# A two-layer gated attention trunk: head transposes through the projections' PSUM banks, attention outputs written over the queries, and a last merge ordered by rows

## The chip, the cores and the metric

The kernel runs on one core of one Trainium2 chip. The metric is the device time of one execution in microseconds; the time of the kernel before is 639.28 us, the median of three runs (639.04 to 639.41). One execution was recorded by the hardware profiler; its own time was 638.95 us.

## The reference

Each of two layers normalises 256 rows of 1024 numbers, projects them by `w_in`, and runs three attention branches beside each other: A (8 heads, causal), B (8 heads, each query sees only the 64 keys that an index score picked) and M (4 heads over 256 memory rows). Each branch is gated, lifted to 1024 columns by its own matrix, weighted by a gate of its own and summed; the sum goes through `w_out` and is added to the rows. All arithmetic is in float32. Cut to its core:

```
proj = einsum('bsd,dc->bsc', rmsnorm(x), w_in)
qa, ka, qb, kb, qi, ki = partial_rope(...)             # first 16 of each head's 64 numbers
ya = moba_attention(qa, ka, va) * silu(a_g)            # one block of 256: plain causal attention
yb = dsa_attention(qb, kb, vb, qi, ki, wi) * silu(b_g) # top 64 keys by index score
ym = memory_attention(m_q, km, vm) * silu(m_g)
up = einsum('bsnw,nwd->bsnd', stack([ya, yb, ym]), w_branch)
x  = x + einsum('bsd,de->bse', sum(sigmoid(mix) * up, axis=2), w_out)
```

## The kernel before

Every float32 product is made of three matmuls (`mm3`, L105 to L108): both operands are split into a rounded part and the rest, and high x high, high x low and low x high are summed in PSUM. Weights come in units of 128x1024 numbers (512 KB): a DMA on SyncE's queue into `raw`, ScalarE rounds it into `whi` (L102), VectorE subtracts to get `wlo` (L103), and TensorE uses a unit in 24 matmuls of 512 columns or 48 of 256. TensorE writes into eight PSUM banks in three pools: `pmm` with four (accumulators of projections, and later of the branch matrices), `psa` with two (scores), `pst` with two (transposes).

The order in a layer is: memory keys and values; the index projection (`index_mask`, L394), whose 584 columns for two row tiles take two banks of `pmm` and two of `psa`; the projections M_Q and M_G; memory attention; A_Q, A_K, A_G, attention A with its values; the same for B; then six mixing projections (`mixes`) and six branch products (`merge`); `merged_T`; `w_out`.

For queries and keys a projection is rotated (`rope`: ScalarE copies, VectorE makes three small products, GpSimd adds them at L207 into `qf`), transposed by TensorE into a bank (`heads_T`, L211 to L219, eight transposes in two banks), and split by ScalarE and VectorE into the tile `dst` (L227). The index keys, queries of A and B and keys of A and B go through `heads_T`; in this kernel its banks are from `pst`.

VectorE also carries the index scores, the 16 turns of top-k (MAX8 and MATCH_REPLACE, L441 and L442), the memory scores' row maxima (L369), the splits of transposed probabilities (L385) and the gating of outputs (L390). The framework's scheduler fixes one order of instructions for each engine ahead of the run; an engine waits in that order, and an accumulator's bank is reused only when its readers are done.

`merge` (L539) adds for each of its two weight units both row tiles into two banks, multiplies by the mix on VectorE (L551), and GpSimd adds that to the sum (L553). `merged_T` transposes the sum (L562) and splits it into `mgh` and `mgl` (L564, L565), the left operands of `w_out`.

Of the kernel before, what the change touches and what calls it, by code (L numbers as in the profile page):

```python
# [7 lines left out]
F32 = mybir.dt.float32  # L8
F32R = mybir.dt.float32r
AF = mybir.ActivationFunctionType  # L10
ALU = mybir.AluOpType
PSUM = bass.MemoryType.PSUM

P = 128
D = 1024
S = 256
# [18 lines left out]
def trunk(ctx, tc, x, x_t, mem, mem_t, consts, norm_g, gains, w_grp, w_idx, w_mix, w_kv, w_br, w_o, final_g, out):  # L35
# [1 line left out]

    cp = ctx.enter_context(tc.tile_pool(name="cp", bufs=1))
    wp = ctx.enter_context(tc.tile_pool(name="wp", bufs=4))
    big = ctx.enter_context(tc.tile_pool(name="big", bufs=9))  # L40
    wk = ctx.enter_context(tc.tile_pool(name="wk", bufs=2))
    pmm = ctx.enter_context(tc.tile_pool(name="pmm", bufs=4, space=PSUM))
    psa = ctx.enter_context(tc.tile_pool(name="psa", bufs=2, space=PSUM))
# [2 lines left out]
    def bank(pool, tag):  # L46
        return pool.tile([P, 512], F32, tag=tag, name=tag)
# [4 lines left out]

    gm = cp.tile([P, 2, L, KC], F32, name="gm")
    nc.sync.dma_start(gm, gains)
    memT = cp.tile([P, KC, S], F32, name="memT")
    xr = [cp.tile([P, D], F32, name=f"xr{t}") for t in range(NT)]
    mr = [wk.tile([P, D], F32, tag="h", name="mr", bufs=3) for t in range(NT)]

# [78 lines left out]
    def mem_stats():  # L137
        nc.vector.tensor_copy(rB, rstd_row(mr, rsm))

    def mem_prep(l, mh, ml, ks):  # L140

        for k in ks:
            g = gm[:, 1, l, k:k + 1]
            nc.scalar.activation(mh[:, k, :], memT[:, k, :], AF.Copy, scale=g)
            nc.vector.scalar_tensor_tensor(ml[:, k, :], memT[:, k, :], g, mh[:, k, :].bitcast(F32),
                                           op0=ALU.mult, op1=ALU.subtract)
# [64 lines left out]
    def heads_T(qf, done):  # L211

        for c in range(2):
            pt = bank(pst, "pt")
            for i in range(2):
                for t in range(NT):
                    j = 2 * c + i
                    nc.tensor.transpose(pt[:, i * S + t * P:i * S + (t + 1) * P], qf[t][:, j * P:(j + 1) * P], ident)  # L218
            done(c, pt.rearrange("p (a b) -> p a b", b=S))  # L219
# [99 lines left out]
    def attn_out(p, prs, v, y, s2):  # L319
        pt0 = bank(pst, "pt").rearrange("p (a b) -> p a b", b=S)  # L320
        pt1 = bank(pst, "pt").rearrange("p (a b) -> p a b", b=S)
        for i in range(2):
            for t in range(NT):
                nc.tensor.transpose(pt0[:, i, t * P:(t + 1) * P], prs[t][:, i, 0:P], ident)  # L324
        for i in range(2):
            nc.tensor.transpose(pt1[:, i, 0:P], prs[1][:, i, P:S], ident)
        h0 = wk.tile([P, 2, S], F32R, tag="ph", name="ph")
        l0 = wk.tile([P, 2, S], F32R, tag="pl", name="pl")
        split(h0, l0, pt0)
        b1 = wk.tile([P, 2, 2, P], F32R, tag="pb", name="pb")  # L330
        split(b1[:, :, 0], b1[:, :, 1], pt1[:, :, :P])
        yf = wk.tile([P, S], F32, tag="yf", name="yf")
        for i, pool in enumerate(((psa, "sc"), (pst, "pt"))):

            yp = bank(*pool)
            c = slice((2 * p + i) * P, (2 * p + i + 1) * P)
            nc.tensor.matmul(yp[:, :S], v[:, 0, c], h0[:, i], start=True, stop=False, skip_group_check=True)
            nc.tensor.matmul(yp[:, :S], v[:, 0, c], l0[:, i], start=False, stop=False, skip_group_check=True)
            nc.tensor.matmul(yp[:, P:P + S], v[:, 1, c], b1[:, i].rearrange("p a b -> p (a b)"), start=False, stop=True,
                             skip_group_check=True)  # L340
            r, q = slice(64 * i, 64 * i + 64), slice(64 - 64 * i, 128 - 64 * i)
            nc.scalar.copy(yf[r], yp[q, :S])
            nc.vector.tensor_add(yf[r], yf[r], yp[r, :S])
            nc.vector.tensor_add(yf[r, P:S], yf[r, P:S], yp[r, S:S + P])
        nc.vector.scalar_tensor_tensor(yf, yf, 0.5, s2[:, p * S:(p + 1) * S], op0=ALU.mult, op1=ALU.mult)
        split(y[:, 0, p * S:(p + 1) * S], y[:, 1, p * S:(p + 1) * S], yf)

    def attend(qT, kT, vals, masks, y, s2):
        prs = attn_probs(0, qT, kT, masks)
        v = vals()  # L350
        for p in range(4):
            ahead = attn_probs(p + 1, qT, kT, masks) if p < 3 else None
            attn_out(p, prs, v, y, s2)
            prs = ahead

    def mem_probs(p, qT, kT):
        prs = []
# [118 lines left out]
    mhl = mem_tiles()  # L476
    for l in range(L):
        if l == 0:
            xT = big.tile([P, KC, S], F32, tag="big", name="xT")
            rest = [[], [], [(xr[0], x[0:P, :])], [(xr[1], x[P:S, :])], [(cst, consts), (xT[:, :4], x_t[:, :4])],  # L480
                    [(xT[:, 4:], x_t[:, 4:])], [], []]

            def ahead(u):
                if u < 4:
                    nc.sync.dma_start(memT[:, 2 * u:2 * u + 2, :], mem_t[:, 2 * u:2 * u + 2, :])
                    mem_prep(l, *mhl, range(2 * u, 2 * u + 2))
                for a, b in rest[u]:
                    load_after(a, b)
                if u > 5:
                    for k in range(4 * u - 24, 4 * u - 20):  # L490
                        nc.scalar.activation(xT[:, k, :], xT[:, k, :], AF.Copy, scale=gm[:, 0, 0, k:k + 1])
                if u == 7:
                    normT.extend(normed_first(xT))
# [26 lines left out]
        aq = roped(l, A_Q, hh, hl, queries_T, "aq")  # L520
        ak = roped(l, A_K, hh, hl, keys_T, "ak")
        gate(l, A_G, hh, hl, s2[0])
        yA = two("yA")
        attend(aq, ak, lambda: values(l, A_V, hh, hl, "av"), cmask, yA, s2[0])

        bq = roped(l, B_Q, hh, hl, queries_T, "bq")
        bk = roped(l, B_K, hh, hl, keys_T, "bk")
        gate(l, B_G, hh, hl, s2[1])
        yB = two("yB")
        attend(bq, bk, lambda: values(l, B_V, hh, hl, "bv"), masks, yB, s2[1])  # L530

        def mixes(b, n):

# [5 lines left out]
        def merge(b, n, mx, acc):  # L539

            ups = [bank(pmm, "mm") for _ in range(NT)]
            for u in range(2):
                hi, lo = unit(w_br[l, b, n, :, 2 * u:2 * u + 2, :], 1024)
                for q in range(2):
                    k = 2 * u + q
                    ww = slice(q * 512, (q + 1) * 512)
                    for t in range(NT):
                        yy = slice(k * S + t * P, k * S + (t + 1) * P)
                        mm3(ups[t], ys[n][:, 0, yy], ys[n][:, 1, yy], hi[:, ww], lo[:, ww], k == 0, k == 3)
            for t in range(NT):  # L550
                nc.vector.scalar_tensor_tensor(mx[:, t], mx[:, t], 1.0, ups[t], op0=ALU.add, op1=ALU.mult)  # L551
                if n:
                    nc.gpsimd.tensor_tensor(acc[:, t], acc[:, t], mx[:, t], op=ALU.add)  # L553

        def merged_T(b, acc):

# [10 lines left out]

        mh = big.tile([P, KC, S], F32R, tag="big", name="mgh")
        ml = big.tile([P, KC, S], F32R, tag="big", name="mgl")
        ys = [yA, yM, yB]  # L570

        todo = [(0, 0), (0, 1), (1, 0), (1, 1), (0, 2), (1, 2)]
        mxs = [mixes(*todo[j]) for j in range(3)]
        for j, (b, n) in enumerate(todo):
            if j == 3 and l + 1 < L:
                mhl = mem_tiles()
                mem_prep(l + 1, *mhl, range(KC))
            merge(b, n, mxs[j], mxs[2 * b])
            if j != 2 and len(mxs) < 6:
                mxs.append(mixes(*todo[len(mxs)]))  # L580
            if n == 2:
                merged_T(b, mxs[2 * b])
# [123 lines left out]
```

## Time and profile before

| what | value |
|---|---|
| median of three runs | 639.28 us |
| profiled execution, its own time | 638.95 us |
| its span, first to last instruction | 637.2 us |
| TensorE busy, share of the span | 615.4 us, 97% |
| VectorE busy | 482.0 us, 76% |
| ScalarE busy | 389.5 us, 61% |
| GpSimd busy | 109.8 us, 17% |

The busy time of TensorE counts matmuls, whose ends are modelled; the weight loads run beside them. The granted clock (PEclk) is 1.00 at 2.4 GHz and 0.50 at 1.2 GHz. In rows of the timeline the first number is the start in us from the span's start, the second the duration; what stands in brackets is the idle time just before, and what ended it. A matmul's own duration is longer than the step to the next one, so the pace of matmuls is read from their starts.

### The profile page before, as it was taken

The page shows a single profiled execution, that of the slowest core. Times are in us where ns is not written, and L with a number is a line of the kernel's source. Part 1 is how long each engine was busy: PE and PEld are TensorE (multiplying, and loading weights), DVE is VectorE, ACT ScalarE, POOL GpSimd, SP SyncE. Part 2 cuts the span into 40 slices and gives each one's busy share as a digit, 9 for nine tenths or more (in the row PEclk, how much of TensorE's full clock was granted, in tenths as well). Part 3 has the DMA queues.
Part 4 walks back from the last instruction along what each step waited for, and adds up shares of the span by engine and source line. Part 5 has one row for each costly group of instructions (what it writes and reads, how often), then busy time and mean ns, then how long its engine had stood idle before and what let it go on. Part 6 is the DMA issues. An engine that isn't in the chain of part 4 may idle for free.

```text
span 637.2 us, 10090 instructions
## 1 busy us (share of the span) xinstructions
PE 615.4 (97%) x3518; PEld 537.9 (84%) x3518; DVE 482.0 (76%) x994; ACT 389.5 (61%) x721; POOL 109.8 (17%) x166
## 2 busy tenths in 40 slices
PE   7989999999999999988999999999999999999795
PEld 4989989889988888867889998998898888888684
DVE  5678799987867878965485777998886688877453
ACT  5858656677756867552464666647765577665232
POOL 1303003013110114304010200210321002312222
PEclk9999999999999999998999999999999999999799
DMA  8966554456455455563554855454555464555421
GB/s 301 372 193 229 180 171 148 130 167 193 141 170 164 162 166 167 172 192 95 178 180 126 269 165 169 136 166 156 174 156 165 135 202 159 170 164 173 125 66 67
DMA packets 31587, 108.52 MB, mean 170 GB/s; under 512 B 3632, under 2 KB 3632, under 8 KB 31536
## 3 DMA queue, kind: packets, MB, share of 16 engines
q1 hardware_dynamic: 31248, 107.35, 52.5%
q8 instruction: 28, 0.46, 0.3%
q10 hardware_dynamic: 288, 0.52, 0.2%
q14 instruction: 23, 0.19, 0.1%
HBM read 106.81 MB, written 1.05 MB: 169 GB/s over the span
## 4 chain that ended last, share of the span: by engine, by line
PE 90%; DVE 3%; DMA 2%; issue 1%; POOL 1%; ACT 1%; SPq 0%; POOLq 0%; DVEq 0%; ACTq 0%
PE mm L107 24%; PE mm L106 24%; PE mm L108 24%; PE sc L106 2%; PE sc L108 2%; PE sc L107 2%; PE sc L298 2%; PE pt L218 1%; DVE wlo L103 1%; PE pt L324 1%; PE pt L106 1%; DMA raw<-in_w_kv 1%; PE pt L108 1%; PE pt L107 1%; PE sc L295 1%
## 5 line engine op out<-in xcount | busy, mean ns | idle before, releaser
L103 DVE TENSOR_TENSOR wlo<-raw,whi 128x1024 fp32r<-128x1024 f32 (+2 forms) x201 | 242.0, 1207 | 95.9 <-ACT whi L102 94.2
L102 ACT CAST whi<-raw 128x1024 fp32r<-128x1024 f32 (+2 forms) x201 | 203.8, 1017 | 138.0 <-PE mm L108 67.4
L108 PE MATMUL mm<-whi,hl 128*128 128x512 f32 (+2 forms) x416 | 159.3, 384 | 1.4 <-DVE hl L103 1.4
L106 PE MATMUL mm<-whi,hh 128*128 128x512 f32 (+2 forms) x416 | 159.9, 387 | 0.0
L107 PE MATMUL mm<-wlo,hh 128*128 128x512 f32 (+2 forms) x416 | 159.9, 385 | 0.0
L108 PEld LDWEIGHTS mm<-whi,hl 128*128 128x128 f32 x416 | 78.0, 188 | 16.0 <-DVE hl L103 1.6
L107 PEld LDWEIGHTS mm<-wlo,hh 128*128 128x128 f32 x416 | 78.2, 188 | 13.4
L106 PEld LDWEIGHTS mm<-whi,hh 128*128 128x128 f32 x416 | 77.9, 188 | 13.5
L285 POOL TENSOR_SCALAR pr<-pr,rinv 128x256 f32<-128x256 f32 (+1 forms) x80 | 45.8, 588 | 172.1 <-DVE rinv L283 148.0
L108 PE MATMUL mm<-hh,wlo 128*128 128x256 f32 x256 | 73.0, 286 | 0.3 <-DVE wlo L103 0.3
L107 PE MATMUL mm<-hl,whi 128*128 128x256 f32 x256 | 72.7, 284 | 0.0
L106 PE MATMUL mm<-hh,whi 128*128 128x256 f32 x256 | 72.7, 284 | 0.0
L108 PEld LDWEIGHTS mm<-hh,wlo 128*128 128x128 f32 x256 | 48.9, 191 | 0.5 <-DVE wlo L103 0.5
L106 PEld LDWEIGHTS mm<-hh,whi 128*128 128x128 f32 x256 | 49.0, 191 | 0.1
L107 PEld LDWEIGHTS mm<-hl,whi 128*128 128x128 f32 x256 | 48.9, 191 | 0.1
L207 POOL TENSOR_TENSOR qf<-rt,rt 128x128 f32<-128x128 f32 (+2 forms) x24 | 17.4, 732 | 175.7 <-DVE rt L206 175.7
L280 ACT ACTIVATE pr<-tm,nb 128x128 f32<-128x128 f32 (+1 forms) x80 | 36.7, 460 | 17.0 <-DVE nb L314 13.8
L553 POOL TENSOR_TENSOR mx<-mx 128x512 f32<-128x512 f32 x16 | 28.2, 1778 | 83.5 <-DVE mx L551 83.5
L536 ACT ACTIVATE mx<-mm 128x512 f32<-128x512 f32 x24 | 14.3, 598 | 10.1 <-PE mm L108 9.8
L106 PE MATMUL mm<-mh,whi 128*128 128x256 f32 x64 | 18.1, 284 | 0.0
L107 PE MATMUL mm<-ml,whi 128*128 128x256 f32 x64 | 18.0, 283 | 0.0
L108 PE MATMUL mm<-mh,wlo 128*128 128x256 f32 x64 | 17.9, 284 | 0.0
(257 smaller groups left out, 1130.7 us busy)
## 6 DMA issues: line engine op xcount, KB each, us to landing
raw<-in_w_grp SPq DMA_DIRECT2D x80, 512.0 KB, 4.5
raw<-in_w_mix SPq DMA_DIRECT2D x48, 512.0 KB, 3.9
raw<-in_w_br SPq DMA_DIRECT2D x24, 512.0 KB, 3.8
raw<-in_w_o SPq DMA_DIRECT2D x16, 512.0 KB, 3.6
raw<-in_w_kv SPq DMA_DIRECT2D x15, 512.0 KB, 4.3
raw<-in_w_idx SPq DMA_DIRECT2D x16, 292.0 KB, 3.2
memT<-in_mem_t SPq DMA_DIRECT2D x4, 256.0 KB, 5.7
xr<-in_x SPq DMA_DIRECT2D x2, 512.0 KB, 6.5
```

Of the source, the lines that this page charges most:

```text
L102: nc.scalar.copy(hi, src)
L103: nc.vector.tensor_sub(lo, src, hi.bitcast(F32))
L106: nc.tensor.matmul(o, lh, rh, start=start, stop=False, skip_group_check=True)
L107: nc.tensor.matmul(o, lh, rl, start=False, stop=False, skip_group_check=True)
L108: nc.tensor.matmul(o, ll, rh, start=False, stop=stop, skip_group_check=True)
L207: nc.gpsimd.tensor_tensor(dst[:, :, 0:16], t1[:, :nh], t2[:, :nh], op=ALU.add)
L218: nc.tensor.transpose(pt[:, i * S + t * P:i * S + (t + 1) * P], qf[t][:, j * P:(j + 1) * P], ident)
L280: nc.scalar.activation(pr[:, i, :nk], tm[:, i, :nk], AF.Exp, bias=nb[:, i:i + 1], scale=scale, accum_out=rsum[:, i:i + 1])
L285: nc.gpsimd.tensor_scalar(pr[:, i, :nk], pr[:, i, :nk], rinv[:, i:i + 1], 1.0, op0=ALU.mult, op1=ALU.mult)
L298: nc.tensor.matmul(scs[i][:, 1, :], qT[:, h, P:], k[:, b, :], start=b == 0, stop=b == 1, skip_group_check=True)
L536: lambda t, i, ps: nc.scalar.activation(mx[:, t], ps, AF.Tanh, scale=0.5))
L553: nc.gpsimd.tensor_tensor(acc[:, t], acc[:, t], mx[:, t], op=ALU.add)
```

## The change

Four edits. `heads_T` takes its two banks from `pmm` in place of `pst`. `attend` has no output tile of its own any more: the output y of head pair p is written into slices 2p and 2p+1 of the query tile, and the pool `big` has ten buffers in place of nine. The transposed memory `memT`, loaded once into a buffer of its own, lies in `big`, and is loaded a second time (1 MB) for layer 1 in the middle of layer 0's merges. `merge` takes both weight units first and does all 12 matmuls of row tile 0 before those of row tile 1, and the sum of the last branch is made on VectorE and not on GpSimd.

```diff
-    big = ctx.enter_context(tc.tile_pool(name="big", bufs=9))
+    big = ctx.enter_context(tc.tile_pool(name="big", bufs=10))
...
-    memT = cp.tile([P, KC, S], F32, name="memT")
...
     def heads_T(qf, done):
         for c in range(2):
-            pt = bank(pst, "pt")
+            pt = bank(pmm, "mm")
...
-        split(y[:, 0, p * S:(p + 1) * S], y[:, 1, p * S:(p + 1) * S], yf)
+        split(y(0, p), y(1, p), yf)
...
-    def attend(qT, kT, vals, masks, y, s2):
+    def attend(qT, kT, vals, masks, s2):
+        def y(part, pair):
+            return qT[:, 2 * pair + part, :]
...
-        yA = two("yA")
-        attend(aq, ak, lambda: values(l, A_V, hh, hl, "av"), cmask, yA, s2[0])
+        yA = attend(aq, ak, lambda: values(l, A_V, hh, hl, "av"), cmask, s2[0])
...
             ups = [bank(pmm, "mm") for _ in range(NT)]
-            for u in range(2):
-                hi, lo = unit(w_br[l, b, n, :, 2 * u:2 * u + 2, :], 1024)
-                for q in range(2):
-                    k = 2 * u + q
-                    ww = slice(q * 512, (q + 1) * 512)
-                    for t in range(NT):
-                        yy = slice(k * S + t * P, k * S + (t + 1) * P)
-                        mm3(ups[t], ys[n][:, 0, yy], ys[n][:, 1, yy], hi[:, ww], lo[:, ww], k == 0, k == 3)
+            us = [unit(w_br[l, b, n, :, 2 * u:2 * u + 2, :], 1024) for u in range(2)]
             for t in range(NT):
+                yy = slice(t * P, (t + 1) * P)
+                for k in range(4):
+                    hi, lo = us[k // 2]
+                    ww = slice(k % 2 * 512, (k % 2 + 1) * 512)
+                    mm3(ups[t], ys[n](0, k)[:, yy], ys[n](1, k)[:, yy], hi[:, ww], lo[:, ww], k == 0, k == 3)
                 nc.vector.scalar_tensor_tensor(mx[:, t], mx[:, t], 1.0, ups[t], op0=ALU.add, op1=ALU.mult)
                 if n:
-                    nc.gpsimd.tensor_tensor(acc[:, t], acc[:, t], mx[:, t], op=ALU.add)
+                    (nc.gpsimd, nc.vector)[n - 1].tensor_tensor(acc[:, t], acc[:, t], mx[:, t], op=ALU.add)
...
             if j == 3 and l + 1 < L:
                 mhl = mem_tiles()
-                mem_prep(l + 1, *mhl, range(KC))
+                memT = big.tile([P, KC, S], F32, tag="big", name="memT")
+                load_after(memT, mem_t)
+                mem_prep(l + 1, memT, *mhl, range(KC))
```

The edits move instructions on every engine. Three places on TensorE follow, each before and now (line numbers of the changed file are smaller by one up to `attend`). First, TensorE behind the index projection in layer 0; `qf` is the rotated index query, `hh` and `hl` are the left operands of M_Q. Before:

```order
L106 MATMUL sc<-whi,hh 128x264
L107 MATMUL sc<-wlo,hh 128x264
L108 MATMUL sc<-whi,hl 128x264
L106 MATMUL mm<-hh,whi 128x256
L107 MATMUL mm<-hl,whi 128x256
...
L107 MATMUL mm<-hl,whi 128x256
L218 MATMUL pt<-cst,qf 128x128
L108 MATMUL mm<-hh,wlo 128x256
```

Now:

```order
L105 MATMUL sc<-whi,hh 128x264
L106 MATMUL sc<-wlo,hh 128x264
L107 MATMUL sc<-whi,hl 128x264
L217 MATMUL mm<-cst,qf 128x128 x2
L105 MATMUL mm<-hh,whi 128x256
L106 MATMUL mm<-hl,whi 128x256
```

Before, 29 matmuls of M_Q stand between the index projection's last matmul and the first transpose of `qf`; now two transposes stand directly behind it, and M_Q behind them. In layer 1 the same two transposes stand at the same place.

Second, TensorE ahead of the gate projection A_G in layer 0. `sc_1131` is the memory output of the second head pair, `qf_1166` and `qf_1286` are rotated A queries and A keys, `mm_1583` before is an accumulator of the values, `mm_1415` now is A_G's first accumulator. Before:

```order
L106 MATMUL sc_1131<-ph_1152,vm_110 128x256
L107 MATMUL sc_1131<-pl_1153,vm_110 128x256
L108 MATMUL sc_1131<-ph_1152,vm_110 128x256
L218 MATMUL pt_1268<-cst_83,qf_1166 128x128 x4
L218 MATMUL pt_1277<-cst_83,qf_1166 128x128 x4
L107 MATMUL mm_1583<-wlo_1605,hh_322 128x512
L108 MATMUL mm_1583<-whi_1604,hl_323 128x512
```

Now:

```order
L217 MATMUL mm_1389<-cst_82,qf_1286 128x128 x3
L217 MATMUL mm_1402<-cst_82,qf_1286 128x128 x3
L106 MATMUL sc_1131<-pl_1138,vm_110 128x256
...
L105 MATMUL sc_1131<-ph_1152,vm_110 128x256
L106 MATMUL sc_1131<-pl_1153,vm_110 128x256
L107 MATMUL sc_1131<-ph_1152,vm_110 128x256
L105 MATMUL mm_1415<-hh_322,whi_1418 128x256
L106 MATMUL mm_1415<-hl_323,whi_1418 128x256
```

Before, A_G and the values run among the memory outputs and the transposes; now A_K (48 matmuls of 512 columns) is the last weight work ahead of the memory outputs and both sets of transposes, and A_G's 96 matmuls come in one piece behind all of them. A_G's first accumulator is the bank that held the first half of the A queries' transposes (`mm_1268`, read by VectorE as below).

```order
L444 MAX m8_1358<-work_710 128x8
L102 TENSOR_TENSOR aq_1267<-mm_1268,aq_1267 64x2x256
L102 TENSOR_TENSOR aq_1267<-mm_1277,aq_1267 64x2x256
L445 MATCH_REPLACE work_709<-m8_1337,work_709 128x128
L102 TENSOR_TENSOR ak_1387<-mm_1389,ak_1387 64x2x256
L102 TENSOR_TENSOR ak_1388<-mm_1402,ak_1388 64x2x256
L445 MATCH_REPLACE work_710<-m8_1358,work_710 128x256
L393 SCALAR_TENSOR_TENSOR yf2_1162<-sc_1131,s2_912 128x512
L102 TENSOR_TENSOR aq_1267<-mm_1268,aq_1267 64x2x256
```

These are VectorE's rows now: the second of the two splits that read `mm_1268` stands behind the top-k turns, the key splits and the gating of `sc_1131`, and A_G's first matmul waits for it.

Third, TensorE at the last merge of the first column half in layer 0. Before:

```order
L107 MATMUL mm<-wlo,yB 128x512
L108 MATMUL mm<-whi,yB 128x512 x2
L562 MATMUL mm<-cst,mx 128x128 x8
L106 MATMUL mm<-whi,yB 128x512
L107 MATMUL mm<-wlo,yB 128x512
```

Now (`bq` is the query tile that holds B's output):

```order
L105 MATMUL mm<-whi,bq 128x512
L106 MATMUL mm<-wlo,bq 128x512
L107 MATMUL mm<-whi,bq 128x512
L562 MATMUL mm<-cst,mx 128x128 x4
L105 MATMUL sc<-whi,mgh 128x512
L106 MATMUL sc<-wlo,mgh 128x512
```

Before, eight transposes of the sum follow the branch product at once; now row tile 0's four follow, 12 matmuls of `w_out` stand behind them, and row tile 1's four come after those.

## Rows read from the trace of the kernel before

**Rows 1.** The page: span, TensorE's busy time, the chain by engine.

```profile
span 637.2 us, 10090 instructions
PE 615.4 (97%) x3518; PEld 537.9 (84%) x3518; DVE 482.0 (76%) x994; ACT 389.5 (61%) x721; POOL 109.8 (17%) x166
PE 90%; DVE 3%; DMA 2%; issue 1%; POOL 1%; ACT 1%; SPq 0%; POOLq 0%; DVEq 0%; ACTq 0%
```

**Rows 2.** Timeline of TensorE, layer 0's last merges: start, duration, instruction, idle before.

```profile
281.38 0.39 PE L107 MATMUL mm<-wlo,yB 128*128 128x512 f32 x1
281.61 0.39 PE L108 MATMUL mm<-whi,yB 128*128 128x512 f32 x1
283.98 0.50 PE L106 MATMUL mm<-whi,yB 128*128 128x512 f32 x1 [1.98 <-ACT yB L102]
...
285.01 0.63 PE L108 MATMUL mm<-whi,yB 128*128 128x512 f32 x2
287.60 0.66 PE L562 MATMUL mm<-cst,mx 128*128 128x128 f32 x4 [1.96 <-POOL mx L553]
289.81 1.11 PE L562 MATMUL mm<-cst,mx 128*128 128x128 f32 x4 [1.55 <-POOL mx L553]
```

**Rows 3.** Timeline of TensorE, layer 1's last merges.

```profile
592.95 0.39 PE L108 MATMUL mm<-whi,yB 128*128 128x512 f32 x1
595.19 0.66 PE L562 MATMUL mm<-cst,mx 128*128 128x128 f32 x4 [1.86 <-POOL mx L553]
597.40 1.12 PE L562 MATMUL mm<-cst,mx 128*128 128x128 f32 x4 [1.55 <-POOL mx L553]
```

**Rows 4.** Windows behind those waits: length, busy times, granted clock, DMA share, GB/s.

```profile
290.00:293.00 3.00, 3.00 (x11) 2.53 (x10) 0.69 (x1) 0.60 (x1) 0.00 (x0) 0.56 0.41 152
597.40:603.00 5.60, 5.60 (x15) 4.55 (x16) 0.69 (x1) 0.60 (x1) 0.00 (x0) 0.50 0.23 84
```

**Rows 5.** Timeline of TensorE: first M_Q matmuls in layer 0, then layer 1.

```profile
45.88 0.28 PE L106 MATMUL mm<-hh,whi 128*128 128x256 f32 x1
...
356.75 0.28 PE L106 MATMUL mm<-hh,whi 128*128 128x256 f32 x1
356.87 0.28 PE L107 MATMUL mm<-hl,whi 128*128 128x256 f32 x1
```

**Rows 6.** Timeline of GpSimd: the index queries' rotation, layer 0, then layer 1.

```profile
48.45 1.27 POOL L207 TENSOR_TENSOR qf<-rt,rt 128x80 f32<-128x80 f32 x1 [15.79 <-DVE rt L206]
49.88 1.20 POOL L207 TENSOR_TENSOR qf<-rt,rt 128x48 f32<-128x48 f32 x1 [0.16 <-DVE rt L206]
...
51.67 0.36 POOL L207 TENSOR_TENSOR qf<-rt,rt 128x80 f32<-128x80 f32 x1 [0.21 <-DVE rt L206]
...
358.73 1.59 POOL L207 TENSOR_TENSOR qf<-rt,rt 128x80 f32<-128x80 f32 x2 [33.23 <-DVE rt L206]
```

**Rows 7.** VectorE by line and shape, 88 to 118 us: busy us, mean ns.

```profile
L103 DVE TENSOR_TENSOR wlo<-raw,whi 128x1024 fp32r<-128x1024 f32 x9 | 10.9, 1215 | 0.8 <-ACT whi L102 0.8
L369 DVE CUSTOM_DVE_ANT_0 tm<-sc,rB 128x256 f32<-128x256 f32 x8 | 3.0, 414 | 0.0
L441 DVE MAX8 m<-work 128x8 f32<-128x256 f32 x7 | 2.9, 414 | 0.0
L385 DVE SCALAR_TENSOR_TENSOR pl<-pt,rsm,ph 128x512 fp32r<-128x512 f32 x4 | 2.9, 736 | 0.0
L442 DVE MATCH_REPLACE8 work<-m,work 128x256 f32<-128x256 f32 x7 | 2.9, 408 | 0.0
L441 DVE MAX8 m<-work 128x8 f32<-128x128 f32 x7 | 2.0, 284 | 0.0
L442 DVE MATCH_REPLACE8 work<-m,work 128x128 f32<-128x128 f32 x7 | 1.9, 275 | 0.0
L390 DVE SCALAR_TENSOR_TENSOR yf<-sc,s 128x512 f32<-128x512 f32 x1 | 0.7, 681 | 0.0
```

**Rows 8.** The same 30 us as one window; columns as in rows 4.

```profile
88.00:118.00 30.00, 30.00 (x206) 27.87 (x206) 29.18 (x96) 17.46 (x34) 6.33 (x14) 1.00 0.49 150
```

More of the change, by code (lines that the diff above doesn't have):

```diff
@@ L138, in mem_stats, with mem_prep @@
         nc.vector.tensor_copy(rB, rstd_row(mr, rsm))
-    def mem_prep(l, mh, ml, ks):
+    def mem_prep(l, memT, mh, ml, ks):
         for k in ks:
@@ L354, in attend @@
             prs = ahead
+        return y
     def mem_probs(p, qT, kT):
@@ L485, in ahead @@
                     nc.sync.dma_start(memT[:, 2 * u:2 * u + 2, :], mem_t[:, 2 * u:2 * u + 2, :])
-                    mem_prep(l, *mhl, range(2 * u, 2 * u + 2))
+                    mem_prep(l, memT, *mhl, range(2 * u, 2 * u + 2))
                 for a, b in rest[u]:
@@ L528, in trunk @@
         gate(l, B_G, hh, hl, s2[1])
-        yB = two("yB")
-        attend(bq, bk, lambda: values(l, B_V, hh, hl, "bv"), masks, yB, s2[1])
+        yB = attend(bq, bk, lambda: values(l, B_V, hh, hl, "bv"), masks, s2[1])
         def mixes(b, n):
@@ L569, in trunk @@
         ml = big.tile([P, KC, S], F32R, tag="big", name="mgl")
-        ys = [yA, yM, yB]
+        ys = [yA, lambda part, k: yM[:, part, k * S:(k + 1) * S], yB]
         todo = [(0, 0), (0, 1), (1, 0), (1, 1), (0, 2), (1, 2)]
@@ L576, in trunk @@
                 mhl = mem_tiles()
-                mem_prep(l + 1, *mhl, range(KC))
+                memT = big.tile([P, KC, S], F32, tag="big", name="memT")
+                load_after(memT, mem_t)
+                mem_prep(l + 1, memT, *mhl, range(KC))
             merge(b, n, mxs[j], mxs[2 * b])
```

## The prediction

> **What bounds the kernel now.** I read the page first: TensorE is busy for 615.4 of 637.2 us and the chain that ends last is 90% TensorE [rows 1]. So what counts is whether an edit opens or closes a gap on TensorE; work on the other engines is free while TensorE has matmuls that can run. The idle time is 22 us. The timeline of TensorE puts part of it at the end of each layer. In layer 0 the matmul after the one at 281.61 starts at 283.98, waiting for the last split of yB; with a pace of 0.23 us (281.38 to 281.61) that is 2.14 us lost. Then 285.47 (two matmuls from 285.01) to 287.60 is 2.13 us, and from the end of four transposes (4 x 0.11 us, an estimate from half of a 256-column step) to 289.81 another 1.77, both waiting for GpSimd's sum L553 [rows 2]. Layer 1 has the last two: 2.01 and 1.77 us [rows 3]. Behind these waits the granted clock is 0.56 of full over 3.0 us and 0.50 over 5.6 us, that is 1.2 GHz and not 2.4 GHz for most of the stretch, which costs 3.0 x 0.44 = 1.3 and 5.6 x 0.5 = 2.8 us [rows 4]. Together 7.4 us in layer 0 and 6.6 in layer 1. The other idle time lies in the first 40 us and the last 10, which the change hardly touches.
>
> **The change part by part.** *Last merges and y over the queries: -12 us.* Now B's attention ends before the branch products need it (the outputs need no tile of their own, and VectorE's last split of y comes before the last mixing products), so the wait for yB goes. The sum is made on VectorE, where an instruction over 128x512 takes 0.68 us [rows 7], and under row tile 0's product and sum (1.4 us) lie row tile 1's 12 matmuls, 2.7 us. So both waits for GpSimd go, and the clock drop with them: -14.0 us. What is late next is the split of row tile 0's four transposes: `w_out`'s 12 matmuls stand right behind them, and 0.4 us of transposes and 0.6 us of ScalarE's copy come ahead. I take 1 us per layer, so -12; bounds -14 and -10. Writing y over the queries costs nothing, since a pair's scores are read long before its y comes.
>
> *Index queries through the projections' banks: +8.5 us.* Before, M_Q's first matmul follows the index projection at once, at 45.88 us [rows 5], and 29 of M_Q cover the rotation. Now the first two transposes stand there, and M_Q takes the banks that the index projection leaves. TensorE can't go past a transpose whose `qf` isn't ready, and GpSimd's order there is the old one: its additions end at 48.45 + 1.27 and 49.88 + 1.20 = 51.08 [rows 6]. So TensorE stands from 45.88 to 51.1, 5.2 us, less 0.3 us that it waited there before: 4.9. In layer 1 M_Q starts at 356.75 [rows 5] and the two additions end at 358.73 + 1.59 = 360.32 [rows 6]: 3.6. What covered this, M_Q, now stands behind it. From below: if GpSimd's additions took the 0.36 us that the same shape takes at 51.67 [rows 6], the second, which can't start before 49.88, ends at 50.24, and the stand is 4.4 - 0.3 = 4.1 and some 2.8 us: 6.9 in all. From above 9.
>
> *A's queries and keys through those banks: +16 us.* This is the large term. Before, A_G and the values run among the memory outputs. Now, from the end of A_Q to A_G, TensorE has only A_K (48 matmuls of 0.23 us = 11.0) and 73 short ones (24 memory scores, 24 memory outputs and transposes, nearly all at 0.12 us or under [rows 5]; about 8.4): 19.4 us. A_G's first matmul waits until VectorE has read the bank of A's queries for the second time. VectorE has, from the first memory score to that split: 5 weight splits of 1.215 us (6.1), 8 row maxima of 0.414 (3.3), 8 MAX8 of 0.284 and 8 of 0.414 (5.6), 8 MATCH_REPLACE of 0.275 and 8 of 0.408 (5.5), 4 splits of 0.736 (2.9), 8 of 0.681 (5.4) [rows 7], and 37 small ones of 0.08 to 0.28 us (4.7): 33.5 us. Neighbours overlap: the 26 groups of that answer, of which eight stand in rows 7, sum to 36.0 us where VectorE was busy for 29.18 of 30 us [rows 8], a factor of 0.81. So 27.2 us, and about 1 us until the first score is there (six matmuls and a hand-over, an estimate), against 19.4: TensorE stands 9 us, in pieces, the largest ahead of A_G. In layer 1 the turns of top-k are fewer at that point: 31.9 x 0.81 = 25.8, plus 1, against 57 x 0.23 + 61 x 0.12 = 20.2; 7 us. Together 16. VectorE was 97% busy over the same work before [rows 8] and TensorE still never stood, because it had A_G and the values to run; that cover is what goes. From below: with VectorE quite caught up the last wait stays, as the gating of the second memory output and the split behind it (2 x 0.681 and hand-overs) come after TensorE's last matmul: 1.5 us per layer, 3 in all. From above: without overlap between neighbours the stand is 33.5 + 1 - 19.4 = 15 in layer 0 and 13 in layer 1; I hold 11 each for the practical end, as GpSimd's and ScalarE's hand-overs lie in between. I take 16, by the row nearest to it, the busy share in rows 8.
>
> *B's queries and keys:* the same transposes there wait for `qf` with weight matmuls of the neighbours in between: +1 per layer, 0 to 2.
>
> *The clock:* behind gaps of about 2 us the trace shows 1.3 and 2.8 us lost to 1.2 GHz [rows 4]. There are four new places with a gap of 3 us or more (two behind the index projection, two ahead of A_G): 4 x 1 = 4 us, bounds 0 and 4 x 2.8 = 11. The Trainium skill ("TensorE: Matmul & The Clock Gate", section "What's actually happening") says that the halved clock is the resting state, which activity lifts and idleness brings back; the trace agrees as far as the two places in rows 4 go. By that rule alone each of the four would be sure to pay.
>
> *Memory in common buffers:* eight ScalarE and eight VectorE instructions in layer 0's merges stay, one GpSimd copy and a 1 MB load come in, on SyncE's queue between weight loads. At the 150 GB/s of rows 8 it takes 7 us; the DMA engines are half idle there [rows 8], and ScalarE reaches the eight instructions some five units after the load is issued. I take 0, bounds 0 and 3.
>
> **Sum**, against the profiled execution (span 637.2 [rows 1] plus 1.75 around it, 638.95): -12 + 8.5 + 16 + 2 + 4 + 0 = +18.5, so 657.4; the median is 0.3 above that execution, so 657.7. I forecast 657.5 us.
>
> **Rivals.**
> - *VectorE is not late.* The stand ahead of A_G is only its last wait, 1.5 us per layer, because VectorE gains its lead while TensorE stands behind the index projection; no clock drop, B at 0. Then -14 + 6.9 + 3 = -4.1: 635 us, faster. It decides once A's part costs under 14 - 6.9 = 7.1 us in both layers together. For it: VectorE has weight splits of A_G in the list that it might do earlier. Against it: memory scores can't be reduced before they are made, and VectorE executes in order, so most of the 33 us can't move ahead of A_Q's end.
> - *Half of A's term.* Stalls of 4 us per layer, since the factor of 0.81 is smaller when more small instructions stand side by side, and no clock drop: -12 + 8.5 + 8 + 2 = +6.5: 645.5 us.
> - *Every gap also drops the clock*, at the dearer price of rows 4, and A's term is 20: -12 + 8.5 + 20 + 2 + 11 = +29.5: 669 us. For it: both waits of about 2 us in a row were followed by 1.2 GHz. Against it: A's stand is split among short matmuls.
> - *The change moves nothing*: the gain at the layers' ends and the loss behind the index projection balance, and A's part is about 4: 639. It needs two sums to meet.
>
> **How the numbers follow.** The forecast (650 to 664): 0.50. Half of A's term (640 to 650): 0.20. Clock drops everywhere (664 to 675): 0.15. VectorE not late: 0.11. Nothing: 0.04. Within 0.2%, 638.0 to 640.6, is about what a measurement of this kernel can't tell from no change. So faster 0.11, same 0.04, slower 0.85. The range 642 to 671 leaves out the two last cases and the far edges of the others, together a little under 0.2.
>
> **What the profile of the changed kernel would show.** Right: TensorE idle for 4 to 5 us and 3 to 4 us ahead of the first `mm<-cst,qf`, with GpSimd's L207 ending it; idle time ahead of A_G's first matmul, ended by VectorE's split into `aq`, with VectorE busy throughout; no wait for L553 and none for yB at the layers' ends; about 1 us ahead of the first `sc<-whi,mgh`; the granted clock 0.5 behind the longest gaps. Wrong: if TensorE runs through the memory outputs with VectorE idle there (A's term falls and the time is below 645), if the waits at the layers' ends remain under another name (the -12 goes, and the time is near 670), or if ScalarE waits for the second load of the memory.

## The result, and the profile after

The changed kernel takes 674.9 us (median of four runs, 674.27 to 677.82) where the kernel before takes 639.16 on the same chip: a ratio of 1.0564, 95% interval 1.0534 to 1.0595. It is slower, as forecast, but by 36 us and not by 18; the range ended at 671. The profiled execution is the longest of the four, 677.82 us, with a span of 676.0 where that of before is 637.2 [rows 1]: 38.8 us to find.

The page of the changed kernel, its span, busy times, and its chain by engine:

```profile
span 676.0 us, 10076 instructions
PE 629.3 (93%) x3518; PEld 548.3 (81%) x3518; DVE 482.5 (71%) x1002; ACT 389.6 (58%) x721; POOL 94.9 (14%) x159
PE 75%; DVE 14%; DMA 3%; issue 3%; ACT 2%; POOL 1%; SPq 0%; POOLq 0%; ACTq 0%; DVEq 0%
```

TensorE has the same 3518 matmuls and is busy 14 us longer, and idle 25 us longer. More busy time for the same instructions goes with a slower clock, which the windows below price; VectorE and ScalarE have what they had. The chain has 15 points less of TensorE, and 11 of them are now VectorE's. What TensorE waited for, in the view of waits (line and releaser: us in all, times, longest):

```profile
PE mm L217 <- POOL qf L206: 19.0, 9, 3.8
PE mm L105 <- DVE aq L102: 7.6, 2, 4.0
PE sc L105 <- ACT mgh L564: 2.4, 2, 1.2
...
PE sc L106 <- DVE pl L388: 1.5, 1, 1.5
...
PE sc L107 <- DVE mgl L565: 1.1, 2, 0.5
```

The transposes of the rotated heads (L217) stand first. The waits for yB and for GpSimd's sum, 8.9 us of idle time before [rows 2, 3], are gone, and 3.5 us for the splits of the merged sum have come. Where the waits lie, in TensorE's timeline:

```profile
48.75 0.33 PE L217 MATMUL mm<-cst,qf 128*128 128x128 f32 x1 [2.84 <-POOL qf L206]
51.68 0.48 PE L217 MATMUL mm<-cst,qf 128*128 128x128 f32 x1 [2.60 <-POOL qf L206]
112.04 1.33 PE L217 MATMUL mm<-cst,qf 128*128 128x128 f32 x8 [1.74 <-POOL qf L206]
114.83 0.58 PE L106 MATMUL sc<-pl,vm 128*128 128x256 f32 x1 [1.47 <-DVE pl L388]
121.56 0.58 PE L105 MATMUL mm<-hh,whi 128*128 128x256 f32 x1 [4.01 <-DVE aq L102]
179.71 0.69 PE L217 MATMUL mm<-cst,qf 128*128 128x128 f32 x2 [3.83 <-POOL qf L206]
...
380.31 0.33 PE L217 MATMUL mm<-cst,qf 128*128 128x128 f32 x1 [1.60 <-POOL qf L206]
381.56 0.47 PE L217 MATMUL mm<-cst,qf 128*128 128x128 f32 x1 [0.92 <-POOL qf L206]
...
448.82 0.38 PE L105 MATMUL mm<-hh,whi 128*128 128x256 f32 x1 [3.63 <-DVE aq L102]
507.05 0.68 PE L217 MATMUL mm<-cst,qf 128*128 128x128 f32 x2 [3.83 <-POOL qf L206]
```

In order: behind the index projection, ahead of A_G, at B's keys, and the same three places in layer 1. Before, M_Q ran at 45.88 and 356.75 where the index waits now stand [rows 5]. And the clock, in windows around these places (length, busy times, granted clock, DMA share, GB/s):

```profile
49.00:57.00 8.00, 5.40 (x28) 5.32 (x28) 3.78 (x19) 2.11 (x7) 2.38 (x5) 0.57 0.63 223
114.00:125.00 11.00, 6.16 (x27) 5.86 (x28) 10.74 (x25) 7.08 (x13) 0.00 (x0) 0.53 0.18 57
179.00:183.00 4.00, 3.29 (x16) 3.29 (x17) 2.28 (x7) 0.00 (x0) 1.93 (x2) 0.57 0.73 245
312.00:316.00 4.00, 3.90 (x13) 3.08 (x13) 0.64 (x2) 0.00 (x0) 0.00 (x0) 0.57 0.59 192
380.00:388.00 8.00, 6.77 (x33) 6.59 (x34) 2.68 (x17) 0.98 (x5) 2.54 (x6) 0.57 0.52 182
449.00:453.00 4.00, 4.00 (x22) 4.00 (x23) 3.81 (x8) 1.86 (x4) 0.00 (x0) 0.57 0.00 0
507.00:511.00 4.00, 3.95 (x20) 3.95 (x21) 1.61 (x4) 0.00 (x0) 1.37 (x1) 0.57 0.79 253
```

Behind each of the six places TensorE ran near 1.2 GHz; busy time times what the clock lacks of 1.00 gives 2.3, 2.9, 1.4, 2.9, 1.7 and 1.7 us, 12.9 in all, and 1.7 at layer 0's end. Against the forecast, in the profiled execution:

| term | forecast | measured |
|---|---|---|
| layers' ends, waits and clock | -12 | 5.2 now, 13.0 before: -7.8 |
| behind the index projection | +8.5 | 5.4 + 2.5 = 8.0 |
| A's queries and keys | +16 | 7.2 + 5.3 = 12.5 |
| B's queries and keys | +2 | 3.8 + 3.8 = 7.7 |
| clock behind the new gaps | +4 | 12.9 |
| sum | +18.5 | 33.3 |

The rows of the index, A and B count waits alone. The last 5.5 us of the 38.8 are in no row of this table: 2.1 us of idle time (24.9 more than before, of which the waits in the table explain 22.8) and 3.4 us of busy time (13.9 more, of which the slow clock explains 12.9 + 1.7 - 4.1 = 10.5). The profile counts a gap from a matmul's modelled end, so each gap is somewhat longer than its bracket; no run took that apart.

### The profile page after: what moved, and what is told of

Same layout as the page of the kernel before. It is cut to its first block, busy times and chain, and to the rows that moved or that the text cites. A ratio compares the mean times of both kernels' runs of the same rounds, so it can differ in the third digit from the quotient of the medians.

```text
span 676.0 us, 10076 instructions
## 1 busy us (share of the span) xinstructions
PE 629.3 (93%) x3518; PEld 548.3 (81%) x3518; DVE 482.5 (71%) x1002; ACT 389.6 (58%) x721; POOL 94.9 (14%) x159
## 3 DMA queue, kind: packets, MB, share of 16 engines
HBM read 107.86 MB, written 1.05 MB: 161 GB/s over the span
## 4 chain that ended last, share of the span: by engine, by line
PE 75%; DVE 14%; DMA 3%; issue 3%; ACT 2%; POOL 1%; SPq 0%; POOLq 0%; ACTq 0%; DVEq 0%
PE mm L105 20%; PE mm L106 20%; PE mm L107 20%; DVE wlo L102 4%; PE sc L107 2%; PE sc L297 2%; PE sc L106 1%; DMA memT<-in_mem_t 1%; PE sc L105 1%; DVE m L444 1%; ACT whi L101 1%; DVE work L445 1%; DMA raw<-in_w_grp 1%; PE mm L217 1%; PE pt L107 1%
## 5 line engine op out<-in xcount | busy, mean ns | idle before, releaser
L105 PE MATMUL mm<-hh,whi 128*128 128x256 f32 x256 | 77.7, 305 | 7.6 <-DVE aq L102 7.6
L107 PE MATMUL mm<-hh,wlo 128*128 128x256 f32 x256 | 77.2, 302 | 0.0
L106 PE MATMUL mm<-hl,whi 128*128 128x256 f32 x256 | 77.0, 301 | 0.0
L105 PEld LDWEIGHTS mm<-hh,whi 128*128 128x128 f32 x256 | 54.0, 212 | 8.1 <-DVE aq L102 8.1
L106 PEld LDWEIGHTS mm<-hl,whi 128*128 128x128 f32 x256 | 53.9, 211 | 0.0
L107 PEld LDWEIGHTS mm<-hh,wlo 128*128 128x128 f32 x256 | 53.9, 210 | 0.0
L217 PE MATMUL mm<-cst,qf 128*128 128x128 f32 x80 | 14.7, 293 | 19.8 <-POOL qf L206 19.0
L206 POOL TENSOR_TENSOR qf<-rt,rt 128x128 f32<-128x128 f32 (+2 forms) x24 | 15.7, 661 | 110.5 <-DVE rt L205 86.4
L217 PEld LDWEIGHTS mm<-cst,qf 128*128 128x128 f32 x80 | 9.5, 144 | 23.0 <-POOL qf L206 22.4
L553 POOL TENSOR_TENSOR mx<-mx 128x512 f32<-128x512 f32 x8 | 15.0, 1879 | 86.4 <-DVE mx L551 86.4
L551 DVE SCALAR_TENSOR_TENSOR mx<-mx,mm 128x512 f32<-128x512 f32 x24 | 16.4, 682 | 3.6 <-PE mm L107 3.5
```

Source lines behind the costliest of these rows:

```text
L105: nc.tensor.matmul(o, lh, rh, start=start, stop=False, skip_group_check=True)
L106: nc.tensor.matmul(o, lh, rl, start=False, stop=False, skip_group_check=True)
L107: nc.tensor.matmul(o, ll, rh, start=False, stop=stop, skip_group_check=True)
L206: nc.gpsimd.tensor_tensor(dst[:, :, 0:16], t1[:, :nh], t2[:, :nh], op=ALU.add)
L553: (nc.gpsimd, nc.vector)[n - 1].tensor_tensor(acc[:, t], acc[:, t], mx[:, t], op=ALU.add)
```

## The experiments

Each was timed beside the kernel before on the same chip (638.8 to 639.3 us there). The first four split the change.

**The bank of the transposes alone.**

```diff
 # the kernel before
-            pt = bank(pst, "pt")
+            pt = bank(pmm, "mm")
```

> The kernel before with one edit: the head transposes take their banks from the projections' pool. Theory 1 (all of the loss is the transposes' place: TensorE's waits for the rotated heads and for A's query bank, and the slower clock behind them): the changed kernel's waits come back without the gain at the layers' ends, 8 us behind the index projections, 13 ahead of A_G, 8 in B, 13 of clock, so about 680 us. Rival (the outputs over the queries, the new merge order or the second memory load bring part of the loss): only 650 to 660 us.

Measured: 674.8 us, ratio 1.0571 (1.0523 to 1.062). This one line is as slow as the whole change. It is under the 680 of theory 1 and far over the rival: at the layers' ends it no longer waits for yB, waits 6.4 us in all for GpSimd's sums, and keeps the clock at 1.00 behind them (rows in the section on why the prediction was wrong). So the other three edits, on top of this line, bring nothing that can be measured.

**The changed kernel with the transposes back in `pst`.**

```diff
 # the changed kernel
-            pt = bank(pmm, "mm")
+            pt = bank(pst, "pt")
```

> The changed kernel with the head transposes back in the transposes' pool; the other three edits stay. Theory 1: none of the waits for rotated heads, and the gain at the layers' ends stays, 9 to 12 us under the kernel before: 627 to 631 us. Rival (the other edits bring part of the loss): 640 to 655 us.

Measured: 635.3 us, ratio 0.9938 (0.9917 to 0.9959). The other edits gain, but 3.5 us and neither the 9 to 12 of theory 1 nor a loss. Its waits of TensorE over the whole run show where the gain went:

```profile
PE mm L562 <- DVE mx L553: 2.3, 1, 2.3
PE sc L105 <- ACT mgh L564: 1.9, 2, 1.2
...
PE sc L107 <- DVE mgl L565: 0.6, 1, 0.6
```

In layer 0 both row tiles' products end within half a microsecond of each other (their last matmuls start at 283.08 and some 0.23 us later). The likely reason is that VectorE's last split of B's output is late, ending at 281.4 us, and that the scheduler has put the matmuls that need it last; no run shows the reason. So row tile 1's matmuls don't cover row tile 0's sum: TensorE waits 2.3 us for VectorE where it waited for GpSimd.

**Only the index transposes back**, and **only A's and B's back**.

```diff
 # the changed kernel; heads_T is handed the name of its tile
-            pt = bank(pmm, "mm")
+            pt = bank(pst, "pt") if name in ('iqT',) else bank(pmm, "mm")
 # and in the other run
+            pt = bank(pst, "pt") if name in ('aq', 'ak', 'bq', 'bk') else bank(pmm, "mm")
```

> The changed kernel with only the index queries' transposes back in the transposes' pool. Theory 1, with the parts adding up: 8.1 us of waits and 5.5 us of clock behind the index projections go, 675 - 13.6 = 661 us. Rival (a bank taken early is paid for later in any case): 670 us or more, the wait shows up at M_Q or ahead of A_G.

> The changed kernel with A's and B's transposes of queries and keys back in the transposes' pool, the index queries' still in the projections'. Theory 1, with the parts adding up: 20 us of waits and 8 us of clock go, about 647 us. Rival (the waits of A and B are VectorE being late whatever bank is used): 660 us or more.

Measured: 670.0 us (1.0482, 1.0465 to 1.05) and 644.5 us (1.0079, 1.0059 to 1.0099). Against 635.3 the index part costs 9.2 us by itself and A's and B's together 34.7; put together they cost 39.6, so the parts overlap a little. The second run is near theory 1. The first lies at the edge of its rival: A's waits grow from 12.5 to 15.5 us when the index's go.

**A alone, and B alone.** The same edit, with the names of the other two in the list.

> The changed kernel with only A's queries and keys transposed through the projections' banks; the index and B transposes go through the transposes' pool, where this kernel stands at 635.3 us. Theory 1 (the parts add up, as the idle time in the run with the index transposes put back has them: 15 us of waits in A, and about 5 us of clock): 655 us. Rival (A's part was right as forecast and the clock stays up where only A waits): 650 us.

> The changed kernel with only B's queries and keys transposed through the projections' banks. Theory 1: TensorE waits 3.8 us in each layer for the rotated B keys, as in the changed kernel, and loses 1.5 to 3 us of clock: 645 to 647 us. Rival (the forecast's 1 us per layer, the rest being late work that A's and the index's waits push in front of B): 637 to 639 us.

Measured: A alone 658.8 us (1.0322, 1.0302 to 1.0341), 23.5 us over 635.3 and above both expectations; B alone 642.65 us (1.0054, 1.0039 to 1.0069), 7.3 us over it and between the two. A alone waits 7.8 us in layer 0 and 7.9 in layer 1, near the forecast's 9 and 7, with some 7 us of clock. These waits lie within memory attention and at the transposes of A's keys, and none is left ahead of A_G.

B costs something without the others, but not at the same place. TensorE's waits there in layer 0:

```profile
142.62 0.44 PE L217 MATMUL mm<-cst,qf 128*128 128x128 f32 x2 [2.06 <-POOL qf L206]
160.86 0.78 PE L323 MATMUL pt<-cst,pr 128*128 128x128 f32 x3 [1.46 <-POOL pr L284]
```

The first is B's queries, the second A's probabilities; B's keys come at 161.73 without a wait. (This execution, 646.0 us, is the longest of the four.) So the 3.8 us per layer for B's keys come only in runs where A's transposes are in the projections' banks too, as in the changed kernel and in the run without the index's. A alone and B alone add up to 30.8 us, the two together cost 34.7.

**Is the clock lost because TensorE stands?** Work that nobody needs, put into the stand behind the index projection:

```diff
 # the run with only the index transposes in pmm
+        pw = bank(pst, "pt")
+        for i in range(20):
+            nc.tensor.matmul(pw[:48, :P], qf[0][:, 16:64], ident, start=True, stop=True)
         qT = queries_T(qf, "iqT")
```

> The run with only the index transposes in the projections' banks (644.5 us, with a halved clock behind both stands and 4.5 us lost to it), and ahead of the first transposes 20 short matmuls whose product nobody uses; they need only what ScalarE has copied by then, and last about 4 us. Theory 1 (the clock falls because TensorE stands): it stays at 2.4 GHz, and the kernel is 3 to 4.5 us faster with the added work, 640 to 641.5 us. Rival (the clock falls for another reason, or the added work delays as much as it saves): 644 to 646 us.

Measured: 644.0 us, ratio 1.0083 (1.0071 to 1.0096): no gain on 644.5. But the windows around the two places, first without the added work, then with it:

```profile
51.00:55.00 4.00, 3.55 (x17) 3.56 (x18) 1.59 (x15) 0.69 (x3) 1.44 (x5) 0.57 0.81 261
362.00:369.00 7.00, 5.78 (x26) 5.49 (x27) 2.84 (x18) 1.06 (x5) 2.63 (x6) 0.51 0.54 197
```

```profile
48.00:57.00 9.00, 8.82 (x77) 8.66 (x78) 6.50 (x25) 5.10 (x13) 2.66 (x6) 1.00 0.73 247
358.00:367.00 9.00, 8.58 (x75) 8.19 (x75) 5.20 (x24) 4.67 (x13) 2.62 (x6) 1.00 0.66 230
```

With TensorE at work the granted clock stays at 1.00 at both places. So here it is the standing that takes it down. The time is hardly better because the 20 matmuls last 4.5 us and M_Q starts later for them: counted from the last matmul of the index projection, by 0.3 us in layer 0 and by 1.5 us in layer 1, where they run on after `qf` is ready at 361.88. M_Q's first 90 matmuls take 3.1 us less in the two layers together, and 1.8 of these go on the later start.

**Is TensorE waiting for the length of VectorE's list in A?**

```diff
 # the run with only A's transposes in pmm
-        between.extend(lambda t=t, r=r: turn(t, r) for r in range(NSEL // 8 + 1) for t in range(NT))
+        between.extend(lambda t=t, r=r: turn(t, r) for r in (0, NSEL // 8) for t in range(NT))
```

> The run with only A's transposes in the projections' banks, and with 2 of the 9 turns of top-k for each row tile: the index mask isn't the reference's. Theory 1 (ahead of A_G TensorE waits for VectorE, whose list is longer than TensorE's; 14 of 18 turns are 9 to 10 us of it): most of A's waits go, 638 to 642 us, and VectorE has idle time there. Rival (what holds TensorE is the order of the banks, GpSimd's additions and the hand-overs, not the length of VectorE's list): 650 us or more.

Measured: 659.1 us (1.0324, 1.0308 to 1.034), where the run with all turns has 658.8. The forecast's reason for its largest term falls. The same 20 us as a window, first with all turns, then with few (VectorE is the third busy time):

```profile
97.00:117.00 20.00, 12.59 (x70) 10.80 (x69) 19.14 (x59) 13.91 (x31) 6.88 (x12) 0.81 0.29 97
97.00:117.00 20.00, 13.01 (x75) 11.12 (x74) 15.68 (x35) 14.10 (x30) 5.12 (x10) 0.85 0.24 83
```

VectorE falls from 96% busy to 78%, and TensorE's waits in layer 0 only from 7.8 to 7.4 us. Rows of the run with few turns, of TensorE, ScalarE and VectorE, and TensorE's first matmul of A_G:

```profile
90.13 0.82 PE L217 MATMUL mm<-cst,qf 128*128 128x128 f32 x6
```

```profile
108.69 1.26 ACT L387 ACTIVATE ph<-pt,rsm 128x512 fp32r<-128x512 f32 x2 [3.41 <-PE pt L384]
...
110.36 1.07 ACT L101 CAST aq<-mm 64x512 fp32r<-64x512 f32 x2
```

```profile
104.57 1.40 DVE L388 SCALAR_TENSOR_TENSOR pl<-pt,rsm,ph 128x512 fp32r<-128x512 f32 x2
...
108.04 0.69 DVE L393 SCALAR_TENSOR_TENSOR yf<-sc,s 128x512 f32<-128x512 f32 x1 [2.00 <-PE sc L107]
109.42 1.41 DVE L388 SCALAR_TENSOR_TENSOR pl<-pt,rsm,ph 128x512 fp32r<-128x512 f32 x2 [0.68 <-ACT ph L387]
...
114.68 1.30 DVE L102 TENSOR_TENSOR aq<-mm,aq 64x512 fp32r<-64x512 f32 x2
```

```profile
115.42 0.58 PE L105 MATMUL mm<-hh,whi 128*128 128x256 f32 x1 [3.63 <-DVE aq L102]
```

Up to 109 us the engines wait for each other in turn: VectorE 2.0 us for TensorE's memory output, ScalarE 3.4 us for TensorE's transposed probabilities. From 109.42 to past 115.42 VectorE works without a pause, at the splits and gatings that its order has there. Among them are the splits of A's queries. Their transposes end at about 91 us, but ScalarE copies them at 110.36, behind the probabilities of the memory, and until VectorE's second split A_G has no bank: TensorE waits 3.63 us. So by these rows it is the order of the copies on ScalarE and VectorE, in a chain of hand-overs, and not the top-k turns; no run changed that order by itself. A_G starts at 115.42 where the run with all turns has 117.40, so the list was worth 2 us there; what comes behind it runs at 1.2 GHz until 121, and by B's scores near 207 us only 0.4 us of that is left. The run was made with A alone; in the changed kernel itself the turns were not taken out.

**The three other edits one by one.** The new merge alone (row tile by row tile, last sum on VectorE), the outputs over the queries alone, the memory in a common buffer with its second load alone, each on the kernel before, with the lines of the change.

> The kernel before with the new merge alone (row tile by row tile, last sum on VectorE). Theory 1 (the last split of yB comes so late that both row tiles end with it, so of the waits at the layers' ends only GpSimd's go, and VectorE's multiply, sum and TensorE's transposes take their place): 635 to 637 us. Rival (the forecast's mechanism, row tile 1's matmuls cover row tile 0's sum): 627 to 630 us.

> The kernel before with the outputs written over the queries, and nothing else. Theory 1 (it frees buffers that nobody waited for): 638 to 640 us, with the same waits at the layers' ends. Rival (it lets B's attention end earlier, so that the wait for yB goes): 634 to 636.5 us.

> The kernel before with the memory in a common buffer and loaded a second time for layer 1, and nothing else. Theory 1 (the load has the time it needs and the queue has room): 638 to 640 us. Rival (ScalarE waits for the 1 MB and weights come late): 641 to 643 us.

Measured: 636.3 us (0.995, 0.9937 to 0.9963); 638.8 us (0.9998, 0.9983 to 1.0014); 636.8 us (0.9965, 0.9952 to 0.9979). The merge gains 2.6 us, as theory 1 has it. The outputs over the queries change nothing: the wait for yB goes, but 1.5 us of new waits and a clock drop come at 216 us. The memory edit fits neither theory: it gains 2.0 us. Its trace has GpSimd's sums as before but no wait for yB. ScalarE waits 1.64 us for the 1 MB, but TensorE has no wait there; that a buffer more in the pool lets B's last outputs be ordered earlier is likely, but no run shows it.

**The next work ahead of the transposes, index.**

```diff
 # the run with only the index transposes in pmm; first() is M_Q's cols_first(...)
+        first()
         qT = queries_T(qf, "iqT")
```

> The run with only the index transposes in the projections' banks (644.5 us), with M_Q's banks asked for, and its matmuls written, ahead of the index queries' transposes. Theory 1 (TensorE stands because nothing it may run is in front of the transposes; which pool lends the bank costs nothing by itself): M_Q's 96 matmuls cover the rotation and both stands go, 635 to 637 us. Rival (two fewer free banks cost the time wherever the transposes stand): 641 us or more.

Measured: 635.9 us (0.9953, 0.9934 to 0.9971), as with all transposes in `pst`. TensorE's timeline in this run, its step from the index projection to M_Q:

```profile
46.30 0.28 PE L107 MATMUL sc<-whi,hl 128*128 128x264 f32 x1
46.42 0.28 PE L105 MATMUL mm<-hh,whi 128*128 128x256 f32 x1
...
58.66 1.04 PE L217 MATMUL mm<-cst,qf 128*128 128x128 f32 x8
```

The bank is still one of the projections' four. What has gone is the place: M_Q asks for its banks first and runs at once, and the eight transposes come at 58.66 without a wait. So the 9 us were the place in TensorE's order, and not the pool by itself.

**The same for A, and for all three.**

```diff
 # A_Q, A_K: project and rotate; then A_G; only then the transposes
         gate(l, A_G, hh, hl, s2[0])
+        aq, ak = aq(), ak()
```

> The run with only A's transposes in the projections' banks (658.8 us), with the gate projection A_G written, and its banks asked for, ahead of A's transposes. Theory 1 (TensorE stood because A_G, the work it could run, was behind the transposes and their bank): A_G's 96 matmuls cover the chain of memory attention, and most of A's waits and clock go, 636 to 640 us. Rival (the chain of hand-overs is later than all the work at hand, and the waits move to the values and the scores of A): 646 us or more.

> The changed kernel, all transposes in the projections' banks, with the next projection asked for ahead of each set of transposes: M_Q ahead of the index queries', A_G ahead of A's, B_G ahead of B's. Theory 1: the waits behind the index projection and in A go, B's go too, 634 to 639 us. Rival (in B the transposes wait for GpSimd whatever stands in front): 642 to 645 us.

Measured: 647.0 us (1.0118, 1.0098 to 1.0138) and 660.1 us (1.032, 1.0301 to 1.034). A's cost falls from 23.5 to 11.7 us: half of it was the missing cover, as theory 1 has it, and half stays, which puts the time on its rival's side. What holds TensorE now is this, in the view of waits between 118 and 122 us:

```profile
PE mm L217 <- DVE s L271: 3.7, 1, 3.7
PE mm L217 <- DVE aq L102: 0.2, 1, 0.2
```

The transposes wait until VectorE has read A_G's accumulator (L271): by this view that bank is the one they get, so with four banks for accumulators and transposes one of the two comes late. No run gave them more banks. In the run with all three, B's transposes wait for L271 too (four waits, 9.6 us in all), and at 660.1 us theory 1 and its rival both fall.

**The two edits that gain.** The merge and the memory together, on the kernel before.

> The kernel before with the new merge and the memory in a common buffer, transposes and outputs as they were. Theory 1 (the two gains of 2.6 and 2.0 us add up): 634 us, under the changed kernel with its transposes put back (635.3). Rival (both gain at the same place, the layers' ends): 636 us.

Measured: 635.5 us (0.9935, 0.992 to 0.995), between the two expectations; the 0.9938 of the changed kernel with its transposes in `pst` can't be told from it. Either beats both kernels.

## Why the prediction was wrong

The direction, the largest places and the first cause were right: the transposes go where nothing covers the rotation, and TensorE, which executes in order, stands there. The size was half of what it should be. Against the profiled execution the clock is 8.9 us short, B 5.7 and the layers' ends 4.2, while A is 3.5 us too dear. By its steps:

- *Behind the index projection*, "+8.5": right in cause and sum. The waits are 5.4 and 2.5 us where 4.9 and 3.6 were forecast, so two errors partly cancel. The part alone costs 9.2 us, clock included, and moving M_Q ahead takes all of it away, which is the cover that the step named.
- *The clock*, "4 x 1 = 4 us": this is the step that failed most. The trace of before had prices of 1.3 and 2.8 us behind the waits at the two layers' ends [rows 4]; I took 1 for each of four places, below both, and the term gives no reason for it. Measured were six places at 1.4 to 2.9 us, 12.9 in all. The added work behind the index projection shows that the standing causes it there. The Trainium skill ("TensorE: Matmul & The Clock Gate", section "What's actually happening") has the halved clock as the resting state, which idleness brings back; the trace agrees at these six places. It isn't certain at every wait. In the run with the bank line alone TensorE waits twice for GpSimd at the end of each layer, and the clock stays at 1.00:

```profile
309.29 0.66 PE L562 MATMUL mm<-cst,mx 128*128 128x128 f32 x4 [1.63 <-POOL mx L553]
311.49 0.66 PE L562 MATMUL mm<-cst,mx 128*128 128x128 f32 x4 [1.55 <-POOL mx L553]
```

```profile
309.00:314.00 5.00, 3.17 (x17) 2.60 (x18) 2.70 (x3) 1.20 (x2) 2.43 (x2) 1.00 0.56 185
```

  Before, two waits of nearly that length, 1.86 and 1.55 us in layer 1, were followed by 1.2 GHz [rows 3, 4].
- *B's queries and keys*, "+1 per layer": failed. In the changed kernel B's keys come 3.8 us late in both layers, since on GpSimd four normalisations of A's probabilities stand ahead of the rotation's sum, and on VectorE three weight splits. GpSimd's and VectorE's rows in the changed kernel:

```profile
175.05 3.73 POOL L284 TENSOR_SCALAR pr<-pr,rinv 128x128 f32<-128x128 f32 x4 [9.91 <-DVE rinv L282]
179.10 0.56 POOL L206 TENSOR_TENSOR qf<-rt,rt 128x128 f32<-128x128 f32 x1 [0.32 <-DVE rt L205]
```

```profile
177.15 1.27 DVE L102 TENSOR_TENSOR wlo<-raw,whi 128x1024 fp32r<-128x1024 f32 x1
178.46 0.29 DVE L203 TENSOR_TENSOR rt<-mm,cst 128x128 f32<-128x128 f32 x1
```

  The first product of the rotation starts at 178.46, the sum at 179.10, 0.32 us after GpSimd is free: both queues were late together. I had counted on "weight matmuls of the neighbours in between" without adding up either queue, as I had for A.
- *A's queries and keys*, "27.2 us against 19.4": the size was near (12.5 us in the changed kernel, 15.7 for A alone, 16 forecast), but by luck, as the reason was mostly wrong. The sign that was named for it came, VectorE busy throughout (19.14 of 20 us with A alone), and proved nothing: with 14 of 18 top-k turns gone the time is the same. It is a chain of hand-overs with no weight work beside it, at whose end, in the changed kernel, the copies of A's queries free A_G's bank. A_G ahead of it takes half away; of the 11.7 us that stay, 7.3 are waits of the transposes for an accumulator's bank.
- *Last merges*, "-12": failed. Taken with the transposes in `pst`, the other edits gain 3.5 us. The mechanism named, row tile 1's matmuls as cover for row tile 0's sum, isn't in that kernel's order in layer 0, and where it is, 1.7 us per layer for the merged sum's splits take its place, not 1. In the changed kernel it is there in both layers, and waits and clock at the layers' ends fall from 13.0 to 5.2 us; but with the bank line alone 6.4 us were left of the 13.0, so little of this is the new merge's.
- *Memory in common buffers*, "0": near in cost, wrong in the reason. ScalarE does wait for the second load, which the prediction had named as a sign of being wrong. ScalarE in the changed kernel, and TensorE behind it:

```profile
286.96 3.31 ACT L143 ACTIVATE mh<-memT,gm 128x256 fp32r<-128x256 f32 x8 [5.14 <-DMA memT<-in_mem_t]
```

```profile
292.56 0.50 PE L106 MATMUL mm<-wlo,hh 128*128 128x512 f32 x1 [0.56 <-DVE wlo L102]
```

  The load is issued at 277.6 us and takes 9.3 us, not 7; rows 8, from which the 7 was worked out, lie at 88 to 118 us and not at the merges. TensorE loses 0.56 us. By itself the edit gains 2.0 us, which no term had.

The high end, 671, left out that all six gaps would pay the clock and that B would wait as A does. The rival that priced the clock at every gap, 669, came nearest, with a chance of 0.15; its 11 us of clock are near the 12.9, but four places at 2.8 us stand for six at about 2, and its 20 us for A are too many. One reading is off without effect: the 0.11 us of a transpose is half of a 512-column step, and not of a 256-column one.

## What to carry to other kernels

An edit that changes which pool a tile's bank comes from can change the order of work: an engine in order with its transposes ahead of its next weights has no cover. At the index projection the same transposes behind those weights cost nothing; in A half of the cost stayed, most of it waits of the transposes for an accumulator's bank. Price each new gap of TensorE as the gap plus the slow matmuls behind it; here the second was 46% of the first (12.9 of 28.2 us), though not every gap paid. And a busy share of 96% doesn't show that the length of an engine's list sets the pace: with the list cut to 78% the time was the same. Look at what the awaited instruction stands behind, on each engine that it passes.

## What the runs showed of the hardware that was not expected

The clock's price was 1.4 to 2.9 us at each of the six new places, whose waits add up to 2.5 to 7.2 us each, while pairs of waits of nearly one length (1.86 and 1.55 us before, 1.63 and 1.55 with the bank line alone) took the clock down in one kernel and not in the other. GpSimd's sum over 128x80 took 0.36 us in the changed kernel at 48.34 us and 1.27 in the one before [rows 6], with the same instructions in the same order: in the slow case VectorE's weight split of 1.2 us runs beside it, in the other VectorE stands for 0.42 us, until 48.69. No run varied this alone, so that the split slows the sum is likely and not shown.
